# Splitting the weights two row blocks at a time in a two-layer RWKV-7 / forgetting-attention kernel on one core

## The chip, the core and the metric

The kernel runs on one core of one Trainium2 chip. The metric is device time in microseconds (us). Where several executions are told of, their median counts. TensorE is written PE (its weight load PEld), VectorE DVE, ScalarE ACT, GpSimd POOL, and SyncE, which issues most of the transfers, SP.

## What is computed

Two layers on 256 frames of 2048 channels in float32: layer 0 mixes over time with RWKV-7, layer 1 with forgetting attention. Behind each stands a SwiGLU with 5632 hidden channels, and a norm ends the program. Cut to what carries the time:

```
x = x + rwkv7_time_mix(rmsnorm(x), ...)      # k, v, r: 2048x2048 each; LoRAs; recurrence over frames; w_o
x = x + swiglu(rmsnorm(x), w_gu[0], w_d[0])  # (silu(h @ gate) * (h @ up)) @ down
x = x + fox_attention(rmsnorm(x), ...)       # w_in: 2048 x (4*2048 + 96); 32 heads; w_o
x = x + swiglu(rmsnorm(x), w_gu[1], w_d[1])
return rmsnorm(x)
```

The recurrence is `S_t = S_{t-1} diag(w_t) + (S_{t-1} a_t) b_t^T + v_t k_t^T, y_t = S_t r_t` for each of 32 heads of 64 channels.

## The kernel before, in words

Weights are far larger than activations, so every large product holds 128x128 pieces of the activations as the stationary operand and streams weights of 128 rows by 512 columns past them. Matmuls take their operands in a shorter format than float32; to lose nothing, each operand is split exactly in two: `wh` is the weight rounded to the short format, `wl` is the rest (`w - wh`), and likewise for activations (`xh`, `xl`). A block of 128x512 weights then costs, for each of the two halves of the frames, three matmuls: `xh*wh`, `xh*wl`, `xl*wh` (L174, L175, L176), six in all.

The class `Stream` runs the weights. Its plan lists all products in order, 1648 blocks in 828 pieces. A piece is what one transfer brings: two blocks (128x1024, 512 KB), or a single block of 97 rows for the eight products of the decay and in-context-rate LoRAs (`w2`, `a2`). `_load` puts a transfer on SP's queue into one of three staging buffers `st`. `_ensure(p)` is called ahead of the matmuls of block p. It splits all blocks up to p + 6, each with one ACT instruction (L148, rounds `st` to `wh`) and one DVE instruction (L149, `wl = st - wh`), into buffers of one block taken from a ring of seven, then asks for the loads three pieces further on. In the attention layer `deepen` adds two more buffers from a pool `wx`, so that the reach there is p + 8. A staging buffer comes free when the DVE has split its second block; a `wh`/`wl` buffer when the last matmul of its block is done.

All other work is written as generators that advance by one step behind every third matmul (`tick`): norms, transposes, the RWKV-7 recurrence in eight units of 128 frames by 8 heads (`prepare`, `solve`, `merge`, `chain`, `post`), and attention head by head. A scheduler then sets the order on each engine, which is kept strictly. In the recurrence `chain` does, twice per unit, a chain of small matmuls with evictions between them: PE L765/L767, ACT L770 (`vu`), PE L773, ACT L775 (`vu`), PE L778/L780, then DVE L785 or L787/L788 (the new state `sv`) and ACT L789 (`Y`).

At the entrance of the attention layer five tiny transfers (L990 `bf`, L993 and L994 `gains`, 0.1 to 0.2 KB each) go on POOL's queue. L995 on the DVE scales `gains`. Two larger ones (L1003, 384 KB each) go on ACT's queue.

Of the kernel before, what the change touches and what calls it, by code (L numbers as in the profile page):

```python
# [8 lines left out]
F32 = mybir.dt.float32  # L9
F32R = mybir.dt.float32r  # L10
BF16 = mybir.dt.bfloat16
AF = mybir.ActivationFunctionType
ALU = mybir.AluOpType
# [4 lines left out]
P = 128  # L18
# [4 lines left out]
N = 64  # L23
# [41 lines left out]
class Stream:  # L65
# [1 line left out]


    NS = 3
    NW = 7  # L70

    def __init__(self, tc, ctx, plan, limit):
        self.nc = tc.nc
# [2 lines left out]
        self.stage = ctx.enter_context(tc.tile_pool(name="stage", bufs=self.NS))  # L76
        self.wp = ctx.enter_context(tc.tile_pool(name="wp", bufs=self.NW))
        self.psm = ctx.enter_context(tc.tile_pool(name="psm", bufs=4, space=PSUM))
# [52 lines left out]
            self.raw[self.loaded] = st  # L131
            self.loaded += 1

    def _ensure(self, p):

        nc = self.nc
        last = min(p + self.NW - 1 + 2 * (self.extra is not None), len(self.blocks) - 1)
        while self.halved <= last:
            i, j, n, rows, end = self.blocks[self.halved]
            self._load(i)  # L140
            st = self.raw[i][:rows, j * n : (j + 1) * n]
            pool = self.wp
            if self.extra is not None:
                self.turn = (self.turn + 1) % (self.NW + 2)
                pool = self.extra if self.turn < 2 else self.wp
            hi = pool.tile([P, 512], F32R, name="wh")
            lo = pool.tile([P, 512], F32R, name="wl")
            nc.scalar.copy(hi[:rows, :n], st)  # L148
            nc.vector.tensor_tensor(lo[:rows, :n], st, hi[:rows, :n].bitcast(F32), op=ALU.subtract)  # L149
            if end:  # L150
                del self.raw[i]
            self.split[self.halved] = (hi, lo)
            self.halved += 1
        i, _, _, _, end = self.blocks[last]
        self._load(i + self.NS - (not end))

    def gemm(self, name, lhs, ready=None):
        nc = self.nc
        got, _, k, n = self.plan.popleft()
        assert got == name, (got, name)  # L160
        kts = -(-k // P)
        ps = [self.psm.tile([P, 512], F32, name="mm") for _ in range(2)]
        for kt in range(kts):
            self._ensure(self.cur)
            hi, lo = self.split.pop(self.cur)
            self.cur += 1
            if ready is not None:
                self.until(lambda: ready(kt))
            rows = min(P, k - kt * P)
            wh, wl = hi[:rows, :n], lo[:rows, :n]  # L170
            xh, xl = lhs(kt)
            for t in range(2):
                c = slice(t * P, (t + 1) * P)
                nc.tensor.matmul(ps[t][:, :n], xh[:rows, c], wh, start=kt == 0, stop=False)  # L174
                nc.tensor.matmul(ps[t][:, :n], xh[:rows, c], wl, start=False, stop=False)  # L175
                nc.tensor.matmul(ps[t][:, :n], xl[:rows, c], wh, start=False, stop=kt == kts - 1)  # L176
                self.tick()
        return ps
# [20 lines left out]
def hybrid_kernel(ctx, tc, const, x, a_norm_g, a_mix, a_w_rkv, a_w0, a_w1, a_w2, a_a0, a_a1, a_a2,  # L199
                  a_g1, a_g2, a_k_k, a_k_a, a_r_k, a_lnx_g, a_lnx_b, a_w_o, b_norm_g, b_w_in, b_b_f,  # L200
                  b_qn_g, b_kn_g, b_on_g, b_w_o, f_norm_g, f_w_gu, f_w_d, final_g, out):
    nc = tc.nc
# [33 lines left out]
    S = Stream(tc, ctx, plan, 4)  # L236
# [89 lines left out]
    with ExitStack() as actx:  # L326
# [5 lines left out]
        with ExitStack() as bctx:  # L332
            st = bctx.enter_context(tc.tile_pool(name="st1", bufs=1))
# [647 lines left out]
    with ExitStack() as bctx:  # L981
        b1 = bctx.enter_context(tc.tile_pool(name="b1", bufs=1))
        b2 = bctx.enter_context(tc.tile_pool(name="b2", bufs=2))
        S.deepen(bctx.enter_context(tc.tile_pool(name="wx", bufs=2)))
        cdram = dram.tile([H, T], F32, name="cdram")
        oT = pair("xa")
        alpha = b1.tile([P, 2, 2 * H], F32, name="alpha")
        cq = b1.tile([P, 2, H], F32, name="cq")
        bf = b1.tile([H, 1], F32, name="bf")
        nc.gpsimd.dma_start(bf[:, :], b_b_f[0][:, None])  # L990
        gains = b1.tile([P, 2], F32, name="gains")
        for j in range(2):
            nc.gpsimd.dma_start(gains[j * N : j * N + N, 0:1], b_qn_g[0][:, None])  # L993
            nc.gpsimd.dma_start(gains[j * N : j * N + N, 1:2], b_kn_g[0][:, None])  # L994
        nc.vector.tensor_scalar(gains[:, 0:1], gains[:, 0:1], N ** -0.5, None, op0=ALU.mult)  # L995
        nc.vector.tensor_scalar(rsh[:, :], rst[:, :], 0.5, None, op0=ALU.mult)

# [324 lines left out]
```

## Time and profile before

| What | Value |
|---|---|
| three timed runs | 2664.91, 2687.72, 2695.59 us; median 2687.72 |
| the profiled execution | 2667.2 us, its span 2665.4 us |
| mean granted TensorE clock in it | 0.989 |
| PE busy | 2624.3 us, 98% of the span, 15256 matmuls |
| DVE, ACT busy | 1677.5 us (63%), 1478.7 us (55%) |
| POOL busy | 87.9 us (3%) |
| transfers | 468.48 MB, 176 GB/s on the mean |

The span is the time from the first to the last instruction of the profiled execution; the 1.8 us that its own time is longer lie around it. A row of instructions names the line, engine and operation, then out<-in, the shape, the count, the busy time, the mean of one in ns, and the idle time of the engine just before with what ended most of it. A row of a table by stretches gives the stretch, its length, the busy time of each engine with the number of instructions started, the granted clock of TensorE (1.00 is full), the share of the 16 DMA engines and the GB/s. Matmuls are pipelined: a busy time counts each from its start to its modelled end, and starts follow each other faster than that.

### The profile page before, as it was taken

The numbers are of one execution on the slowest core, as the hardware profiler recorded it, in microseconds if no ns is written. First come the engines' busy times: TensorE is split into PE (matmuls) and PEld (weight loads), VectorE is DVE, ScalarE is ACT, GpSimd is POOL, SyncE is SP. The second block draws the span as 40 slices with busy tenths as digits, with TensorE's granted clock in tenths as the row PEclk, the third lists the DMA queues.
The fourth block names the chain that finished last, engine by engine and source line by source line (L and its number), as shares of the span: only waits on it lengthen the run. The fifth ranks groups of instructions, "written<-read, shape, count | busy, mean of one in ns | idle before, by whom it ended". The sixth has DMA issues, their size and how long they took to land.

```text
span 2665.4 us, 41151 instructions
## 1 busy us (share of the span) xinstructions
PE 2624.3 (98%) x15256; PEld 2142.5 (80%) x15256; DVE 1677.5 (63%) x2977; ACT 1478.7 (55%) x2849; POOL 87.9 (3%) x68
## 2 busy tenths in 40 slices
PE   7999999999999999999999999999999999999998
PEld 6788777777888888888888888888888888888886
DVE  7885876766655555555556677776755555555554
ACT  6665676756655545444445565665655555454443
POOL 0000010000000000000000110110000000000000
PEclk9999998889999999999999999999999999999999
DMA  5676332323666666665557666665566666665554
GB/s 187 193 215 206 99 100 79 92 91 111 178 194 185 193 187 191 187 193 191 192 191 205 202 193 184 196 185 170 174 192 186 192 187 191 187 191 193 196 195 157
DMA packets 253946, 468.48 MB, mean 176 GB/s; under 512 B 22248, under 2 KB 32696, under 8 KB 253744
## 3 DMA queue, kind: packets, MB, share of 16 engines
q1 hardware_dynamic: 251056, 464.58, 57.5%
q8 instruction: 120, 1.97, 0.3%
q10 hardware_dynamic: 2528, 1.26, 0.2%
q14 instruction: 82, 0.67, 0.1%
q0 software_dynamic: 160, 0.00, 0.0%
HBM read 457.37 MB, written 4.23 MB: 173 GB/s over the span
## 4 chain that ended last, share of the span: by engine, by line
PE 95%; ACT 2%; DVE 1%; DMA 1%; issue 1%; SPq 0%; ACTq 0%; POOLq 0%; DVEq 0%
PE mm L174 28%; PE mm L176 28%; PE mm L175 28%; PE bg L611 1%; PE bg L765 1%; PE bg L767 1%; DMA st<-in_a_w_rkv_dram 1%; PE bg L941 1%; ACT xb L592 1%; PE bg L773 1%; PE bg L302 1%; PE bg L778 1%; PE bg L780 0%; ACT Bs L811 0%; PE bg L1174 0%
## 5 line engine op out<-in xcount | busy, mean ns | idle before, releaser
L149 DVE TENSOR_TENSOR wl<-st,wh 128x512 fp32r<-128x512 f32 (+1 forms) x1648 | 1130.2, 691 | 823.1 <-ACT wh L148 817.8
L148 ACT CAST wh<-st 128x512 fp32r<-128x512 f32 (+1 forms) x1648 | 1018.8, 623 | 944.9 <-DVE wl L149 695.7
L174 PE MATMUL mm<-wh,xb 128*128 128x512 f32 x2048 | 803.6, 392 | 0.0
L176 PE MATMUL mm<-wh,xb 128*128 128x512 f32 x2048 | 799.8, 391 | 0.0
L175 PE MATMUL mm<-wl,xb 128*128 128x512 f32 x2048 | 799.4, 390 | 0.0
L174 PEld LDWEIGHTS mm<-wh,xb 128*128 128x128 f32 x2048 | 384.6, 188 | 79.9 <-issue 3.3
L176 PEld LDWEIGHTS mm<-wh,xb 128*128 128x128 f32 x2048 | 384.4, 188 | 79.5
L175 PEld LDWEIGHTS mm<-wl,xb 128*128 128x128 f32 x2048 | 384.7, 188 | 76.0
L174 PE MATMUL mm<-wh,xa 128*128 128x512 f32 x768 | 311.2, 406 | 0.0
L175 PE MATMUL mm<-wl,xa 128*128 128x512 f32 x768 | 307.4, 400 | 0.7 <-DVE wl L149 0.7
L176 PE MATMUL mm<-wh,xa 128*128 128x512 f32 x768 | 306.0, 399 | 0.0
L174 PE MATMUL mm<-wh,hb 128*128 128x512 f32 x448 | 174.3, 389 | 0.0
L175 PE MATMUL mm<-wl,hb 128*128 128x512 f32 x448 | 174.3, 389 | 0.0
L176 PE MATMUL mm<-wh,hb 128*128 128x512 f32 x448 | 174.3, 389 | 0.0
L174 PEld LDWEIGHTS mm<-wh,xa 128*128 128x128 f32 x768 | 146.4, 191 | 30.4 <-issue 1.0
L176 PEld LDWEIGHTS mm<-wh,xa 128*128 128x128 f32 x768 | 146.2, 191 | 30.4 <-DVE xa L854 0.2
L175 PEld LDWEIGHTS mm<-wl,xa 128*128 128x128 f32 x768 | 146.6, 191 | 29.2 <-DVE wl L149 1.5
L175 PEld LDWEIGHTS mm<-wl,hb 128*128 128x128 f32 x448 | 84.1, 188 | 17.5
L174 PEld LDWEIGHTS mm<-wh,hb 128*128 128x128 f32 x448 | 84.1, 188 | 17.4
L176 PEld LDWEIGHTS mm<-wh,hb 128*128 128x128 f32 x448 | 84.1, 188 | 17.4
L1122 POOL TENSOR_TENSOR n<-n,pw 128x8 f32<-128x8 f32 x24 | 45.1, 1882 | 411.4 <-DVE n L1121 411.4
L315 DVE TENSOR_TENSOR x<-mm,x 128x512 f32<-128x512 f32 x58 | 38.0, 685 | 11.6 <-PE mm L176 11.5
(277 smaller groups left out, 2007.7 us busy)
## 6 DMA issues: line engine op xcount, KB each, us to landing
st<-in_f_w_gu_dram SPq DMA_DIRECT2D x352, 512.0 KB
st<-in_f_w_d_dram SPq DMA_DIRECT2D x176, 512.0 KB
st<-in_b_w_in_dram SPq DMA_DIRECT2D x128, 512.0 KB
st<-in_a_w_rkv_dram SPq DMA_DIRECT2D x96, 512.0 KB
st<-in_a_w_o_dram SPq DMA_DIRECT2D x32, 512.0 KB
st<-in_b_w_o_dram SPq DMA_DIRECT2D x32, 512.0 KB
x<-in_x_dram SPq DMA_DIRECT2D x16, 256.0 KB
cb<-cdram SPq DMA_DIRECT2D x4, 1024.0 KB
```

The lines of the kernel that those rows point to most:

```text
L148: nc.scalar.copy(hi[:rows, :n], st)
L149: nc.vector.tensor_tensor(lo[:rows, :n], st, hi[:rows, :n].bitcast(F32), op=ALU.subtract)
L174: nc.tensor.matmul(ps[t][:, :n], xh[:rows, c], wh, start=kt == 0, stop=False)
L175: nc.tensor.matmul(ps[t][:, :n], xh[:rows, c], wl, start=False, stop=False)
L176: nc.tensor.matmul(ps[t][:, :n], xl[:rows, c], wh, start=False, stop=kt == kts - 1)
L302: nc.tensor.transpose(tp[:, i * T + t * P : i * T + (t + 1) * P], src[:, t, c : c + P], ident)
L315: nc.vector.tensor_tensor(X[g][:, t, :], ps[t][:, :], X[g][:, t, :], op=ALU.add)
L592: nc.scalar.copy(dst, tpv[half[q], :, c, :])
L611: mm(pm[:, h * P : (h + 1) * P], fkb[us, b * 4 + h, :], far[us, b * 4 + h, :], start=True, stop=True)
L765: mm(pb[us, hs], M[:, c * 8 + h, C : 2 * C], sv[:, hs], start=True, stop=True)
L767: mm(pb[vs, hs], far[us, h, 0:C], sv[us, hs], start=h == 0, stop=False)
L1122: nc.gpsimd.tensor_tensor(n8[:, :], n8[:, :], pw[:, :], op=ALU.pow)
```

## The change

1. A split instruction takes a whole piece: 128x1024 in one ACT and one DVE instruction. `_ensure(i)` now goes by pieces; it is called ahead of each block of piece i and splits up to piece i + 3, then asks for the load of piece i + 6.
2. The ring holds four buffers of 128x1024 (`NW = 4`) where it held seven of 128x512. In the attention layer one more of that size is added where there were two small ones.
3. The five tiny transfers at the attention layer's entrance go on ACT's queue.
4. The program is built with `dynamic_dma_scratch_size=1024`, a smaller ring for POOL's transfers.

```diff
-    NW = 7
+    NW = 4
...
-    def _ensure(self, p):
+    def _ensure(self, i):
...
-        last = min(p + self.NW - 1 + 2 * (self.extra is not None), len(self.blocks) - 1)
+        last = min(i + self.NW - 1 + (self.extra is not None), len(self.pieces) - 1)
         while self.halved <= last:
-            i, j, n, rows, end = self.blocks[self.halved]
-            self._load(i)
-            st = self.raw[i][:rows, j * n : (j + 1) * n]
+            self._load(self.halved)
+            _, _, cnt, n, rows = self.pieces[self.halved]
+            st = self.raw.pop(self.halved)[:rows, : cnt * n]
...
-            hi = pool.tile([P, 512], F32R, name="wh")
-            lo = pool.tile([P, 512], F32R, name="wl")
-            nc.scalar.copy(hi[:rows, :n], st)
-            nc.vector.tensor_tensor(lo[:rows, :n], st, hi[:rows, :n].bitcast(F32), op=ALU.subtract)
+            hi = pool.tile([P, 1024], F32R, name="wh")
+            lo = pool.tile([P, 1024], F32R, name="wl")
+            nc.scalar.copy(hi[:rows, : cnt * n], st)
+            nc.vector.tensor_tensor(lo[:rows, : cnt * n], st, hi[:rows, : cnt * n].bitcast(F32), op=ALU.subtract)
...
-        i, _, _, _, end = self.blocks[last]
-        self._load(i + self.NS - (not end))
+        self._load(last + self.NS)
...
-            self._ensure(self.cur)
-            hi, lo = self.split.pop(self.cur)
+            i, j, _, _, end = self.blocks[self.cur]
+            self._ensure(i)
+            hi, lo = self.split[i]
+            if end:
+                del self.split[i]
...
-            wh, wl = hi[:rows, :n], lo[:rows, :n]
+            wh, wl = hi[:rows, j * n : (j + 1) * n], lo[:rows, j * n : (j + 1) * n]
...
-        S.deepen(bctx.enter_context(tc.tile_pool(name="wx", bufs=2)))
+        S.deepen(bctx.enter_context(tc.tile_pool(name="wx", bufs=1)))
...
-        nc.gpsimd.dma_start(bf[:, :], b_b_f[0][:, None])
+        nc.scalar.dma_start(bf[:, :], b_b_f[0][:, None])
...
-            nc.gpsimd.dma_start(gains[j * N : j * N + N, 0:1], b_qn_g[0][:, None])
-            nc.gpsimd.dma_start(gains[j * N : j * N + N, 1:2], b_kn_g[0][:, None])
+            nc.scalar.dma_start(gains[j * N : j * N + N, 0:1], b_qn_g[0][:, None])
+            nc.scalar.dma_start(gains[j * N : j * N + N, 1:2], b_kn_g[0][:, None])
...
-    nc = _bacc.Bacc("TRN2", target_bir_lowering=False, num_devices=1)
+    nc = _bacc.Bacc("TRN2", target_bir_lowering=False, num_devices=1, dynamic_dma_scratch_size=1024)
```

Because the scheduler sets the order anew, instructions move on every engine. Three places matter below.

The first is ACT at the start of the program, from the last statistics of the input (L281) to the first rounded activations `xa` (L363), on which the first matmuls of the weights wait. L380 evicts the transposed input. Before:

```order
L281 ACTIVATE jk_138,ss<-x_81 128x512
L148 CAST wh<-st 128x512 x4
L380 ACTIVATE hT<-bg,gcol 128x256 x2
L148 CAST wh<-st 128x512 x2
L380 ACTIVATE hT<-bg,gcol 128x256 x4
L363 CAST xa_148<-xmf 128x256
L148 CAST wh<-st 128x512
```

and with the change:

```order
L281 ACTIVATE jk_138,ss<-x_81 128x512
L148 CAST wh<-st 128x1024 x2
L380 ACTIVATE hT<-bg,gcol 128x256 x2
L148 CAST wh<-st 128x1024
L380 ACTIVATE hT<-bg,gcol 128x256 x5
L148 CAST wh<-st 128x1024
L363 CAST xa_148<-xmf 128x256 x3
```

Six blocks stood ahead of the first `xa`, and now eight (four pairs), with one more L380.

The second is ACT in one step of the recurrence, from the eviction of the row weights `wc` (L539) through the chain's evictions L770, L775 and L789. Before:

```order
L539 ACTIVATE wc<-bg 64x8 x2
L844 COPY x_4127<-bg 128x4x128
L871 COPY gt_4667<-mm 128x512
L770 COPY vu<-bg 64x512
L548 ACTIVATE WW<-WW 128x512
L775 COPY vu<-bg 64x512
L148 CAST wh<-st 128x512 x5
L789 COPY Y<-bg 64x512
```

and with the change:

```order
L539 ACTIVATE wc<-bg 64x8 x2
L844 COPY x_3767<-bg 128x4x128
L871 COPY gt_4295<-mm 128x512
L770 COPY vu<-bg 64x512
L548 ACTIVATE WW<-WW 128x512
L148 CAST wh<-st 128x1024
L775 COPY vu<-bg 64x512
L148 CAST wh<-st 128x1024
L789 COPY Y<-bg 64x512
```

Here a pair has moved in front of L775. Over the whole recurrence, of the 48 evictions L770, L775 and L789, 29 stood directly behind a split before, and 19 do now.

The third is ACT at the entrance of the attention layer. With the change:

```order
L148 CAST wh<-st 128x1024 x19
L990 DMA bf<-in_b_b_f_dram 32x1
L281 ACTIVATE jk_12650,ss<-x_6992 128x512
L281 ACTIVATE jk_12652,ss<-x_6992 128x512
L993 DMA gains<-in_b_qn_g_dram 64x1
L994 DMA gains<-in_b_kn_g_dram 64x1
L993 DMA gains<-in_b_qn_g_dram 64x1
L994 DMA gains<-in_b_kn_g_dram 64x1
L148 CAST wh<-st 128x1024 x2
L1003 DMA cb<-in_b_w_in_dram 128x8x96 x2
```

The five tiny transfers stood on POOL between two norms; now they stand on ACT, ahead of the next two pairs.

More of the change, by code (lines that the diff above doesn't have):

```diff
@@ L132, in _load @@
             self.loaded += 1
-    def _ensure(self, p):
+    def _ensure(self, i):
         nc = self.nc
-        last = min(p + self.NW - 1 + 2 * (self.extra is not None), len(self.blocks) - 1)
+        last = min(i + self.NW - 1 + (self.extra is not None), len(self.pieces) - 1)
         while self.halved <= last:
-            i, j, n, rows, end = self.blocks[self.halved]
-            self._load(i)
-            st = self.raw[i][:rows, j * n : (j + 1) * n]
+            self._load(self.halved)
+            _, _, cnt, n, rows = self.pieces[self.halved]
+            st = self.raw.pop(self.halved)[:rows, : cnt * n]
             pool = self.wp
             if self.extra is not None:
-                self.turn = (self.turn + 1) % (self.NW + 2)
-                pool = self.extra if self.turn < 2 else self.wp
-            hi = pool.tile([P, 512], F32R, name="wh")
-            lo = pool.tile([P, 512], F32R, name="wl")
[L148 to L151, printed above, removed]
+                self.turn = (self.turn + 1) % (self.NW + 1)
+                pool = self.wp if self.turn else self.extra
+            hi = pool.tile([P, 1024], F32R, name="wh")
+            lo = pool.tile([P, 1024], F32R, name="wl")
+            nc.scalar.copy(hi[:rows, : cnt * n], st)
+            nc.vector.tensor_tensor(lo[:rows, : cnt * n], st, hi[:rows, : cnt * n].bitcast(F32), op=ALU.subtract)
             self.split[self.halved] = (hi, lo)
             self.halved += 1
-        i, _, _, _, end = self.blocks[last]
-        self._load(i + self.NS - (not end))
+        self._load(last + self.NS)
     def gemm(self, name, lhs, ready=None):
```

## The prediction

> **What bounds the kernel now.** I read the stages first: the table by stretches, one row each for the products k and v with the start (to 250 us), the recurrence (to 655), the first SwiGLU (to 1415), attention (to 1900), the second SwiGLU (to 2653) and the end.
>
> ```profile
> 0.00:250.00 250.00, 230.02 (x1109) 190.56 (x1110) 189.29 (x399) 151.70 (x313) 4.18 (x10) 0.99 0.66 201
> 250.00:655.00 405.00, 395.93 (x4946) 305.29 (x4946) 291.85 (x621) 275.29 (x679) 32.98 (x25) 0.94 0.31 95
> 655.00:1415.00 760.00, 759.91 (x3422) 626.67 (x3421) 428.28 (x643) 388.43 (x652) 0.70 (x1) 1.00 0.63 190
> 1415.00:1900.00 485.00, 484.99 (x2406) 397.94 (x2405) 346.83 (x690) 283.24 (x575) 48.59 (x30) 1.00 0.63 191
> 1900.00:2653.00 753.00, 753.00 (x3379) 622.03 (x3378) 416.84 (x620) 376.07 (x624) 0.70 (x1) 1.00 0.62 187
> 2653.00:2665.00 12.00, 0.41 (x2) 0.00 (x0) 4.42 (x10) 3.96 (x8) 0.70 (x1) 0.74 0.47 175
> ```
>
> The columns are PE, PEld, DVE, ACT, POOL, then the clock. From 655 to 2653 us PE stands for 0.1 us in 1998. But a busy time counts modelled ends, so "busy" doesn't yet say that PE sets the pace: a PE that is fed too slowly could look the same. The timeline of the first SwiGLU, PE, ACT and DVE, seems to say just that:
>
> ```profile
> 1199.55 0.69 DVE L149 TENSOR_TENSOR wl<-st,wh 128x512 fp32r<-128x512 f32 x1 [0.67 <-ACT wh L148]
> 1199.83 0.39 PE L176 MATMUL mm<-wh,hb 128*128 128x512 f32 x1
> 1200.06 0.39 PE L174 MATMUL mm<-wh,hb 128*128 128x512 f32 x1
> ...
> 1200.26 0.62 ACT L148 CAST wh<-st 128x512 fp32r<-128x512 f32 x1 [0.73 <-DVE wl L149]
> ...
> 1200.91 0.69 DVE L149 TENSOR_TENSOR wl<-st,wh 128x512 fp32r<-128x512 f32 x1 [0.67 <-ACT wh L148]
> ...
> 1201.19 0.39 PE L176 MATMUL mm<-wh,hb 128*128 128x512 f32 x1
> ...
> 1201.62 0.62 ACT L148 CAST wh<-st 128x512 fp32r<-128x512 f32 x1 [0.73 <-DVE wl L149]
> ```
>
> ACT, DVE, ACT alternate without a gap in 1201.62 - 1200.26 = 1.36 us, and the six matmuls of a block, L176 to L176, take 1201.19 - 1199.83 = 1.36 us too. If the split were the limit, wider splits would speed up three quarters of the program. The counts decide between the two. Up to 900 us these starts of L174, then of L148:
>
> ```profile
> 0.00:900.00 900.00, 343.95 (x857) 163.20 (x858) 0.97 0.50 150
> 0.00:900.00 900.00, 267.55 (x435) 0.97 0.50 150
> ```
>
> 857 L174 at two per block mean that block 429 is in work; split 435 is in work. Six ahead is all that seven buffers allow, so the splits wait for PE to free a buffer, and the DVE named there only ended at the same moment. PE's own pace, 1.36/6 = 0.227 us per matmul, sets these stages, and the change leaves every matmul as it is: 1648 blocks x 1.36 = 2241 us of the 2665 can't move. Who waits on PE for a split at all is one row in the whole list of waits:
>
> ```profile
> PE mm L175 <- DVE wl L149: 0.7, 1, 0.7
> ```
>
> What remains open is 0 to 250 us, the recurrence with 405 - 395.9 = 9.1 us of idle PE and a mean clock of 0.94, and the entrances of stages.
>
> **The change part by part.** *The price of a pair.* The trace holds a DVE operation of 128x1024, and for ACT casts of two widths:
>
> ```profile
> L149 DVE TENSOR_TENSOR wl<-st,wh 128x512 fp32r<-128x512 f32 x1640 | 1124.7, 691 | 820.9 <-ACT wh L148 815.6
> L1215 DVE TENSOR_TENSOR cb<-cb,cst 128x1024 f32<-128x1024 f32 x8 | 9.7, 1207 | 4.1 <-DMA cb<-cdram 4.1
> L148 ACT CAST wh<-st 128x512 fp32r<-128x512 f32 x1640 | 1013.9, 623 | 942.5 <-DVE wl L149 694.2 <-PE mm L176 183.6 <-DMA st<-in_b_w_in_dram 33.2
> L1011 ACT CAST qT<-cb 128x768 fp32r<-128x768 f32 x2 | 1.6, 843 | 0.0
> ```
>
> DVE: about 1207 ns for a pair against 2 x 691 = 1382, 175 saved. ACT: 843 - 623 = 220 ns per 256 columns, so 1063 for 1024 against 1246, 183 saved. With 820 pairs the busy time falls by 144 us on the DVE and 150 us on ACT. Back to back less is gained, since durations overlap there:
>
> ```profile
> 1485.37 3.09 DVE L149 TENSOR_TENSOR wl<-st,wh 128x512 fp32r<-128x512 f32 x5
> 1481.31 2.70 ACT L148 CAST wh<-st 128x512 fp32r<-128x512 f32 x5
> ```
>
> (3.09 - 0.69)/4 = 0.60 and (2.70 - 0.62)/4 = 0.52 us from start to start, that is 0.09 and 0.10 hidden per instruction, and about 0.08 us saved per pair on each.
>
> *Steady stages (655 to 2653 us): 0.* PE hides all of it. Does the new ring still feed PE? A split began six blocks = 8.16 us ahead of its use and took 0.62 + 0.69 + 0.03 = 1.34: 6.8 us to spare. A pair begins three pieces of 2.72 us ahead, 8.16 again, and takes 1.063 + 1.207 + 0.03 = 2.30: 5.9 us. A staging buffer, once split, has the rest of its round of three pieces for its next load: 8.16 - 2.30 = 5.9 us, where it was 8.16 - 1.36 - 1.34 = 5.5. Both covers hold; if a load came 1 us late every piece, the ring would be empty after six pieces and each further piece would cost that 1 us.
>
> *The start: +1.2 us.* The first matmuls of k wait for `xa` behind the splits on ACT and DVE:
>
> ```profile
> 15.85 1.14 ACT L148 CAST wh<-st 128x512 fp32r<-128x512 f32 x2 [1.22 <-DMA st<-in_a_w_rkv_dram]
> 19.74 1.14 ACT L148 CAST wh<-st 128x512 fp32r<-128x512 f32 x2
> 20.77 1.58 ACT L380 ACTIVATE hT<-bg,gcol 128x256 f32<-128x256 f32 x4
> 22.21 0.43 ACT L363 CAST xa<-xmf 128x256 fp32r<-128x256 f32 x1
> ...
> 23.18 0.48 PE L174 MATMUL mm<-wh,xa 128*128 128x512 f32 x1
> ```
>
> Six blocks stood ahead of that L363, now four pairs and one L380 more: on ACT 4 x 1.063 - 6 x 0.623 = +0.5, and an L380 of 0.4; on the DVE 4 x 1.207 - 6 x 0.691 = +0.7, and two small operations. That gives 0.9 to 1.5 us. From below, 0 (ACT has idle time there, waiting for the load); from above +3, both engines in a row.
>
> *The recurrence: +2 us.* The rows of L148 and of L149 in 250 to 655 us:
>
> ```profile
> 250.00:655.00 405.00, 68.46 (x114) 0.94 0.31 95
> 250.00:655.00 405.00, 76.31 (x113) 0.94 0.31 95
> ```
>
> 114 splits, 8 of them the single blocks of `w2` and `a2`, become 53 pairs and 8 singles: 53 x 0.183 = 9.7 us less on ACT, 53 x 0.175 = 9.3 less on the DVE, which are busy 275 and 292 us there. That is 3% less queueing, and of PE's 9.1 idle us 3% is 0.3. Against it each pair is a longer obstacle. ACT's evictions of the chain wait for PE, not for ACT:
>
> ```profile
> ACT vu L770 <- PE bg L767: 36.4, 11, 6.0
> ACT vu L775 <- PE bg L773: 26.3, 16, 4.0
> ACT Y L789 <- PE bg L780: 16.9, 10, 4.7
> ```
>
> so splits fill holes. By the order, 29 of the 48 stood directly behind a split, 29 x 0.62 = 18.0 us at most; now 19, 19 x 1.063 = 20.2: +2.2. I take the sum, +2. From below: all idle goes, -9. From above, the second rival, +38.
>
> *The entrance of attention: 0.* On POOL the tiny transfers cost a wait on the DVE:
>
> ```profile
> 1415.63 0.69 POOL L990 DMA_DIRECT2D bf<-in_b_b_f_dram x1 [728.95 <-DVE wl L149]
> 1423.58 0.15 DVE L995 TENSOR_SCALAR gains<-gains 128x1 f32<-128x1 f32 x1 [3.64 <-DMA gains<-in_b_qn_g_dram]
> gains<-in_b_qn_g_dram POOLq DMA_DIRECT2D x2, 0.2 KB, 5.5
> 1416.66 0.39 ACTq L1003 DMA_DIRECT2D cb<-in_b_w_in_dram  x1
> ```
>
> On ACT five issues of 0.39 us, 2.0 us in all, delay the two pairs behind them; `bf` also waits there until its space is free, which came at 1415.6, when the first SwiGLU ended. The stall of 3.6 us on the DVE goes or shrinks. The 5.9 us in front of PE cover the 2.0. Without that cover 2 us would be lost, and if weight loads on SP had to wait for these transfers to land (5.5 us by that row), 5.5. Below, nothing: PE has no gap there to win. POOL's smaller ring has no user left.
>
> The sum: 2665.4 + 1.2 + 2 + 0 = 2668.6 us of span, 2670.4 of time, 3 us over the profiled execution. That one lies 20 us under the median of the timed runs, which spread over 31 us by themselves. The middle of all four executions is (2667.2 + 2687.7) / 2 = 2677.5; with the 3 us, **2681 us**. About 1% is what a measurement of this kernel can tell from no change, and this is 0.3%.
>
> **The rivals.** *Faster: the recurrence tightens (2648 us).* If lighter ACT and DVE queues let the chain run without gaps, PE's 9 idle us go, and the clock could stay full: 0.94 over 405 us is 24 us. Together -33. For it: DVE and ACT are 72% and 68% busy there. Against: 3% less load is little, and the clock falls where PE is over 97% busy:
>
> ```profile
> 350.00:400.00 50.00, 48.96 (x674) 1.00 0.36 111
> 400.00:450.00 50.00, 49.20 (x611) 0.87 0.22 70
> 500.00:550.00 50.00, 49.12 (x560) 0.73 0.24 73
> ```
>
> The Trainium skill (TensorE: Matmul & The Clock Gate, Part 1: The HAM clock gate) has the clock at half after an idle window of about 3.4 us. These rows don't show such idleness: 0.8 us of 50 at a clock of 0.87, 1.0 us at 1.00. By that rule fewer gaps would win the 24 us; by the rows nothing ties the two.
>
> *Slower: pairs in front of the chain (2719 us).* The recurrence is one chain through PE, ACT and DVE in order. If every step of it found a pair ahead, 48 evictions would come 1.063 - 0.623 = 0.44 us later, 21 us, and 16 state updates on the DVE, two instructions each, 0.52 us per instruction, 17 us: +38. It takes a loss of 27 us, seven steps in ten, to be 1% slower. Against: 19 evictions stand behind a pair, not 48. The Trainium skill (Perfetto Trace Analysis, Optimizing Scalar/DVE Operations) says that where ACT and DVE aren't saturated but cause bubbles on others, breaking instructions up may let work end sooner; that speaks against pairs here. The trace agrees on the first half only: they aren't saturated, and PE's bubbles are 9 us in 405.
>
> *The split was the limit after all (2585 us).* Were the alternation of 1.36 us what paces PE, pairs at 2.30 per 2.72 us would free up to 0.21 us per block, over the 1376 blocks of attention and the SwiGLUs 289 us in the extreme; a third of it, 96 us, would give 2585. The counts (six ahead, the full ring) exclude it but for a misreading.
>
> **How the numbers follow.** My forecast, no change that can be measured: 0.74. The faster recurrence 0.13, the split as limit 0.02: faster 0.15. The pairs in the way 0.11: slower. The predicted time is the forecast's, 2681. Its own range: below, -9 of the recurrence; above, 3 + 2 + 5.5 = 11 of the parts; and the four executions lie from 13 us below their middle to 18 above it. If all goes one way that is 2677.5 - 9 - 13 = 2656 to 2677.5 + 11 + 18 = 2706. Below I reach on to the first rival's 2648; the slower rival's 2719 and the split as limit stay outside.
>
> **What would show it.** Right: L148 and L149 at 128x1024 with about 1060 and 1210 ns, 820 of each; the stages from 655 to 2653 us as long as before within 3 us; six L174 to L176 still in 1.36 us; splits counted in blocks still 6 to 8 ahead of L174. The first L174 at about 24.3 us (before 23.2). DVE L995 waiting less. Wrong: a stretch of the SwiGLUs shorter by tens of us (then the split was the limit), waits of PE on `wh` or `wl` in the steady stages (then the ring is too short), or a recurrence off 405 us by more than 10 at the same clock.

## The result: 0.8% slower, with the largest loss in attention, where the forecast had none

| | before | after |
|---|---|---|
| median of 20 runs each | 2674.78 us (2664.91 to 2695.59) | 2695.57 us (2681.19 to 2713.26) |
| ratio after/before, 95% interval | | 1.0077 [1.0056, 1.0099] |
| profiled execution, its span, granted clock | 2667.2, 2665.4 us, 0.989 | 2692.75, 2691.0 us, 0.985 |
| DVE, ACT busy | 1677.5, 1478.7 us | 1570.1, 1331.6 us |

The median rose by 20.8 us; the forecast had 3 on top of its base.

**A measure without the clock.** Runs of one kernel lie 30 us apart, so stages can't be compared by length alone. The product of span and mean granted clock helps; it is called the product below. Two runs of the changed kernel had spans of 2679.4 and 2711.5 us at mean granted clocks of 0.989 and 0.978: span times clock is 2650 and 2652. Over its 20 runs the product has a median of 2650.2 (2646 to 2657); over 96 runs of the kernel before, taken beside the experiments, 2636.9 (2632 to 2640). (One more execution of the kernel before, of 8386.67 us, is left out.) The runs of one kernel thus differ by the clock and by little else, and with it taken out the change costs 13.3 us. The rest of the 20.8 lies in the mean clock (0.9839 against 0.9854, 4 us of span) and in the scatter of medians. Below, "clock-free" is a length less the time that a clock under 1 took from it (at half clock, half the time).

The table by stretches, first two rows of the kernel before (recurrence and attention), cut where the first matmul of the same block starts in both kernels. The columns are PE, PEld, DVE, ACT, POOL, the clock, DMA share and GB/s:

```profile
253.00:657.70 404.70, 395.54 (x4946) 304.67 (x4945) 293.02 (x623) 275.86 (x680) 32.98 (x25) 0.94 0.31 95
...
1415.20:1923.40 508.20, 508.19 (x2519) 416.69 (x2518) 364.37 (x721) 300.03 (x612) 48.59 (x30) 1.00 0.63 190
```

and the stages of the changed kernel behind the start: the products of layer 0, the recurrence, the first SwiGLU, attention, the second SwiGLU:

```profile
24.50:253.70 229.20, 224.56 (x1072) 185.46 (x1071) 171.98 (x299) 128.51 (x218) 3.42 (x5) 0.99 0.65 198
253.70:666.30 412.60, 399.57 (x4945) 308.66 (x4943) 292.84 (x571) 270.36 (x629) 34.85 (x25) 0.93 0.31 95
666.30:1424.60 758.30, 758.27 (x3408) 626.84 (x3409) 382.59 (x365) 332.73 (x375) 0.70 (x1) 1.00 0.62 189
1424.60:1948.20 523.60, 515.52 (x2519) 420.11 (x2518) 349.05 (x561) 274.94 (x452) 45.55 (x25) 0.99 0.61 185
1948.20:2677.20 729.00, 729.00 (x3260) 603.24 (x3260) 357.88 (x326) 308.83 (x326) 0.70 (x1) 1.00 0.62 187
```

| stage | before, clock-free | after, clock-free | difference | lost to the clock, before and after |
|---|---|---|---|---|
| first matmul of the weights to the recurrence | 228.1 | 227.4 | -0.7 | 1.7, 1.7 |
| recurrence | 380.8 | 383.7 | +2.9 | 23.9, 29.0 |
| first SwiGLU | 757.5 | 758.3 | +0.8 | 0, 0 |
| attention | 508.3 | 518.5 | +10.2 | 0, 5.1 |
| second SwiGLU | 728.5 | 728.9 | +0.4 | 0, 0 |

With the first matmul, 1.3 us later (23.2 to 24.5 us), the stages of these two executions differ by 14.9; the product gave 13.3 over all runs. Attention holds two thirds of it: DVE and ACT are less busy there than before, by 15 and 25 us, and PE, which stood for 0.01 us in 508, now stands for 523.60 - 515.52 = 8.1.

**Where PE stands.** The list of waits in attention of the changed kernel (engine, line, releaser: total, times, longest), rows left out:

```profile
ACT wh L148 <- DMA st<-in_b_w_in_dram: 57.9, 40, 4.8
...
ACT sc L1165 <- DVE nm L1164: 48.1, 16, 7.3
...
DVE k L1127 <- POOL n L1122: 13.6, 8, 1.8
ACT wh L148 <- DMA st<-in_b_w_o_dram: 11.3, 8, 3.0
DVE x L1127 <- POOL n L1122: 11.3, 8, 1.8
...
DVE o L1127 <- POOL n L1122: 7.9, 5, 1.8
...
PE bg L1174 <- ACT sc L1165: 6.3, 10, 2.4
```

and the same rows of the kernel before:

```profile
ACT wh L148 <- DMA st<-in_b_w_in_dram: 33.2, 24, 3.0
ACT sc L1165 <- DVE nm L1164: 26.6, 15, 2.0
...
DVE x L1127 <- POOL n L1122: 6.1, 8, 1.8
...
DVE k L1127 <- POOL n L1122: 4.1, 5, 1.1
...
ACT wh L148 <- DMA st<-in_b_w_o_dram: 3.6, 3, 1.9
...
DVE o L1127 <- POOL n L1122: 2.3, 5, 0.9
```

Splits now wait 69.2 us for their loads, where it was 36.8. PE isn't stopped by a missing split, though, but by attention's own work: L1174 transposes the scores that L1161, L1164 (DVE) and L1165 (ACT) make. How a late load gets there is read from the timeline of the changed kernel, ACT, DVE and PE ahead of the longest stop:

```profile
1741.89 1.05 ACT L148 CAST wh<-st 128x1024 fp32r<-128x1024 f32 x1 [1.64 <-DMA st<-in_b_w_in_dram]
```
```profile
1742.97 1.23 DVE L149 TENSOR_TENSOR wl<-st,wh 128x1024 fp32r<-128x1024 f32 x1 [1.46 <-ACT wh L148]
1744.12 0.74 DVE L1161 SCALAR_TENSOR_TENSOR sc<-bg,cq,cb 128x128 f32<-128x128 f32 x2
1744.97 1.23 DVE L149 TENSOR_TENSOR wl<-st,wh 128x1024 fp32r<-128x1024 f32 x1
1746.11 0.60 DVE L1164 TENSOR_REDUCE nm<-sc 128x1 f32<-128x128 f32 x2
```
```profile
1746.43 0.40 ACT L1165 ACTIVATE sc<-sc,nm 128x128 f32<-128x128 f32 x1 [1.49 <-DVE nm L1164]
```
```profile
1746.97 0.33 PE L1174 MATMUL bg<-cst,sc 128*128 128x128 f32 x1 [2.40 <-ACT sc L1165]
```

The load is late by 1.64 us, the ACT split with it, the DVE's split behind that by 1.46, and L1161 stands behind it in the DVE's order; L1164 then stands behind one more pair, and PE stops for 2.40 us. Why was the load late? Some 40 us earlier the DVE stood three times for POOL, with splits queued behind (DVE's timeline, then ACT's):

```profile
1697.35 0.69 DVE L1127 TENSOR_TENSOR x<-x,n 128x512 f32<-128x512 f32 x1 [1.53 <-POOL n L1122]
...
1698.67 0.17 DVE L1121 TENSOR_SCALAR n<-n 128x8 f32<-128x8 f32 x1
1700.66 0.69 DVE L1127 TENSOR_TENSOR k<-k,n 128x512 f32<-128x512 f32 x1 [1.81 <-POOL n L1122]
1701.27 1.22 DVE L149 TENSOR_TENSOR wl<-st,wh 128x1024 fp32r<-128x1024 f32 x1
...
1705.49 0.69 DVE L1127 TENSOR_TENSOR k<-k,n 128x512 f32<-128x512 f32 x1 [1.82 <-POOL n L1122]
```
```profile
1694.73 1.05 ACT L148 CAST wh<-st 128x1024 fp32r<-128x1024 f32 x1 [1.31 <-DMA st<-in_b_w_in_dram]
```

The pair that ACT rounded from 1694.73 on was finished by the DVE at 1701.27 + 1.22 = 1702.49: 7.8 us in which its staging buffer couldn't be filled again, against 2.30 without anything between. So the transfers fell to half their rate, two loads of 512 KB short in 12 us, and when they ran again splits stood waiting for them (the table by stretches, its last columns DMA share and GB/s; then ACT's timeline, and SP's):

```profile
1697.00:1703.00 6.00, 6.00 (x30) 4.97 (x29) 3.80 (x7) 1.66 (x3) 1.95 (x2) 1.00 0.27 84
1703.00:1709.00 6.00, 5.73 (x27) 4.45 (x26) 4.15 (x7) 2.55 (x5) 1.64 (x1) 1.00 0.34 93
1709.00:1715.00 6.00, 6.00 (x28) 4.95 (x27) 3.04 (x4) 4.98 (x7) 0.00 (x0) 1.00 0.81 261
```
```profile
1719.91 1.05 ACT L148 CAST wh<-st 128x1024 fp32r<-128x1024 f32 x1 [3.41 <-DMA st<-in_b_w_in_dram]
1724.52 1.05 ACT L148 CAST wh<-st 128x1024 fp32r<-128x1024 f32 x1 [3.56 <-DMA st<-in_b_w_in_dram]
```
```profile
1714.27 0.53 SPq L1096 DMA_DIRECT2D prev<-v  x1
...
1718.20 0.54 SPq L1098 DMA_DIRECT2D prev<-v  x1
```

These two waits have a second part: between the loads SP also issues attention's own transfers `prev<-v`, about as many bytes as one load. The loads that it issued at 1713.85 and 1716.26 us came only at 1719.9 and 1724.5, after 6 and 8 us. The kernel before has the same transfers, and beside them waits of 1.48 and 1.94 us.

ACT waits of 1.5 us for loads go on from there to the late one at 1741.89. The starts, counted as in the prediction, show one lasting shortage: the splits were 8 blocks ahead of the matmuls at 1694.8 us, 5 at 1708.6, 4 at 1724.6, and no more than 6 until PE stopped. In the same part of the kernel before (1680 to 1726 us) they stayed 7 to 9 ahead.

Why does the DVE stand longer for POOL, 32.8 us in its three rows against 12.5? Each of 24 steps is L1121 on the DVE, L1122 on POOL, then L1127 on the DVE. If they are matched in order, a split stands between L1121 and its L1127 in 22 of the 24 before, and in 8 now. A split in that place costs the DVE little, since it would stand for POOL anyway. The step at 1698.67 above has nothing between; one from the kernel before:

```profile
1481.25 0.16 DVE L1121 TENSOR_SCALAR n<-n 128x8 f32<-128x8 f32 x1
...
1482.04 0.68 DVE L149 TENSOR_TENSOR wl<-st,wh 128x512 fp32r<-128x512 f32 x1
...
1483.16 0.69 DVE L1127 TENSOR_TENSOR k<-k,n 128x512 f32<-128x512 f32 x1 [0.36 <-POOL n L1122]
```

That POOL's waits began this shortage is read from the trace; no run takes them away alone. Behind the stop the clock is at half for 10.2 us, the 5.1 us of the table:

```profile
1748.00:1751.40 3.40, 2.70 (x8) 2.00 (x8) 1.30 (x2) 2.14 (x8) 0.00 (x0) 0.50 0.65 183
1751.40:1758.20 6.80, 6.80 (x27) 5.48 (x27) 1.62 (x3) 0.98 (x1) 0.00 (x0) 0.53 0.44 138
```

The theory for the experiments: with three staging buffers and pairs, loads come late in attention, and the late splits hold up attention's own work in the strict order. Its rivals: the moved transfers or POOL's ring (run 1 against 2), the longer reach in attention (run 8), and a cause in the clock, by way of the shorter reach of the ring (runs 9 and 10).

### The profile page after: what moved, and what is told of

It is laid out like the page before. It is cut to its first block, busy times and chain, and to the rows that moved or that the text cites. A ratio compares the mean times of both kernels' runs of the same rounds, so it can differ in the third digit from the quotient of the medians.

```text
span 2691.0 us, 38804 instructions
## 1 busy us (share of the span) xinstructions
PE 2636.5 (98%) x15256; PEld 2152.9 (80%) x15256; DVE 1570.1 (58%) x2157; ACT 1331.6 (49%) x2029; POOL 86.8 (3%) x63
## 4 chain that ended last, share of the span: by engine, by line
PE 84%; DVE 5%; DMA 5%; ACT 3%; issue 2%; POOL 1%; SPq 0%; ACTq 0%; POOLq 0%; DVEq 0%
PE mm L174 25%; PE mm L176 24%; PE mm L175 24%; DVE wl L149 2%; DMA st<-in_b_w_in_dram 2%; PE bg L611 1%; PE bg L765 1%; POOL n L1122 1%; ACT wh L148 1%; PE bg L767 1%; DMA cb<-cdram 1%; PE bg L941 1%; DMA st<-in_a_w_rkv_dram 1%; PE bg L773 1%; ACT xb L592 1%
## 5 line engine op out<-in xcount | busy, mean ns | idle before, releaser
L149 DVE TENSOR_TENSOR wl<-st,wh 128x1024 fp32r<-128x1024 f32 (+1 forms) x828 | 1008.0, 1218 | 887.2 <-ACT wh L148 885.4
L148 ACT CAST wh<-st 128x1024 fp32r<-128x1024 f32 (+1 forms) x828 | 866.8, 1048 | 1024.7 <-PE mm L176 908.1
L174 PE MATMUL mm<-wh,xb 128*128 128x512 f32 x2048 | 806.7, 394 | 0.0
L175 PE MATMUL mm<-wl,xb 128*128 128x512 f32 x2048 | 798.7, 390 | 1.3 <-DVE wl L149 1.3
L174 PEld LDWEIGHTS mm<-wh,xb 128*128 128x128 f32 x2048 | 385.2, 188 | 80.2 <-issue 4.0
L175 PEld LDWEIGHTS mm<-wl,xb 128*128 128x128 f32 x2048 | 385.4, 188 | 78.9 <-DVE wl L149 2.7
L174 PE MATMUL mm<-wh,xa 128*128 128x512 f32 x768 | 312.4, 407 | 1.5 <-ACT xa L853 1.5
L175 PE MATMUL mm<-wl,xa 128*128 128x512 f32 x768 | 306.8, 399 | 2.6 <-DVE wl L149 2.5
L174 PE MATMUL mm<-wh,hb 128*128 128x512 f32 x448 | 174.3, 389 | 0.0
L175 PE MATMUL mm<-wl,hb 128*128 128x512 f32 x448 | 174.3, 389 | 0.0
L174 PEld LDWEIGHTS mm<-wh,xa 128*128 128x128 f32 x768 | 147.0, 191 | 32.7 <-ACT xa L853 1.9
L175 PEld LDWEIGHTS mm<-wl,xa 128*128 128x128 f32 x768 | 147.3, 192 | 31.4 <-DVE wl L149 3.3
L175 PEld LDWEIGHTS mm<-wl,hb 128*128 128x128 f32 x448 | 84.1, 188 | 17.5
L174 PEld LDWEIGHTS mm<-wh,hb 128*128 128x128 f32 x448 | 84.1, 188 | 17.3
L1122 POOL TENSOR_TENSOR n<-n,pw 128x8 f32<-128x8 f32 x24 | 44.9, 1869 | 430.9 <-DVE n L1121 430.9
```

What stands on the lines that cost most here:

```text
L148: nc.scalar.copy(hi[:rows, : cnt * n], st)
L149: nc.vector.tensor_tensor(lo[:rows, : cnt * n], st, hi[:rows, : cnt * n].bitcast(F32), op=ALU.subtract)
L1122: nc.gpsimd.tensor_tensor(n8[:, :], n8[:, :], pw[:, :], op=ALU.pow)
```

## The experiments

Medians are of 8 to 12 runs. The ratios against the kernel before, with their 95% interval, are not the quotients of the medians (its own lie there from 2674.9 to 2676.5 us; in run 4 the medians give 1.0058 and the ratio is 1.0038). The product of span and clock stands beside each median, since it separates 3 us where the median can't.

**1. The transfers alone.** The kernel before, with parts 3 and 4 of the change.

```diff
-        nc.gpsimd.dma_start(bf[:, :], b_b_f[0][:, None])
+        nc.scalar.dma_start(bf[:, :], b_b_f[0][:, None])
...
-    nc = _bacc.Bacc("TRN2", target_bir_lowering=False, num_devices=1)
+    nc = _bacc.Bacc("TRN2", target_bir_lowering=False, num_devices=1, dynamic_dma_scratch_size=1024)
```

> The kernel before with only the five tiny transfers moved to ACT's queue and POOL's ring smaller; splits stay 128x512 in seven buffers. The change measured 1.0077 of before. If wide splits are the cause (width), 0.998 to 1.002 of before and attention (first to last block of its products, 800 to 1120 in the count of blocks, 508 us before, 523.6 in the change) within 2 us of before. If the transfers or their order on ACT are the cause, 1.004 or more.

Measured: 2677.35 us, 1.0003 [0.9971, 1.0035]; product 2635.0; attention 507.6 clock-free. The transfers and the ring cost nothing.

**2. The pairs with the transfers on POOL.** The changed kernel with the five transfers back on POOL's queue.

```diff
-        nc.scalar.dma_start(bf[:, :], b_b_f[0][:, None])
+        nc.gpsimd.dma_start(bf[:, :], b_b_f[0][:, None])
...
```

> The change with the five tiny transfers back on POOL's queue (the smaller ring stays, for space). Width, late loads or buffers by pairs as the cause: 1.005 to 1.010 of before, attention over 516 us. The transfers as the cause: 0.998 to 1.002.

Measured: 2696.47 us, 1.0082 [1.0053, 1.0111]; product 2650.3; attention 517.8. The whole loss is there without the moved transfers: it comes from the pairs.

**3. Half-width splits in buffers of a pair.** The changed kernel; each piece is split in two instructions of 512 on ACT and two on the DVE, and all else stays by pairs.

```diff
-            nc.scalar.copy(hi[:rows, : cnt * n], st)
-            nc.vector.tensor_tensor(lo[:rows, : cnt * n], st, hi[:rows, : cnt * n].bitcast(F32), op=ALU.subtract)
+            for c in [slice(j * n, (j + 1) * n) for j in range(cnt)]:
+                nc.scalar.copy(hi[:rows, c], st[:, c])
+                nc.vector.tensor_tensor(lo[:rows, c], st[:, c], hi[:rows, c].bitcast(F32), op=ALU.subtract)
```

> The change, but each piece is split by two ACT and two DVE instructions of 128x512 into its buffer of 128x1024; reach and release by pieces stay. If the width of an instruction that others stand behind is the cause: 0.998 to 1.003 of before. If buffers that come free by pairs, or the reach counted in pieces, are the cause: 1.005 to 1.010, as the change.

Measured: 2693.16 us, 1.0053 [1.0027, 1.0078]; product 2644.9; attention by stretches, and its waits for loads (lines from there on are one number higher):

```profile
1448.70:1958.10 509.40, 508.23 (x2519) 417.33 (x2518) 360.62 (x721) 290.62 (x612) 41.89 (x25) 1.00 0.62 190
```
```profile
ACT wh L149 <- DMA st<-in_b_w_in_dram: 40.4, 27, 3.8
```

PE's idle time in attention falls from 8.1 to 1.2 us and the stage to 509.4, although DVE and ACT are 12 and 16 us busier in it: there the width of the instruction, with the order that goes with it, makes the difference. Over the whole kernel only 5 of the 13 us of the product come back, and by the ratio the second theory's forecast came true, so the width isn't all (the profiled execution has a product of 2640, at the low end of its runs). The mean clock of 0.983 keeps the median high.

**4. Four staging buffers.** The changed kernel with one more.

```diff
-    NS = 3
+    NS = 4
```

> The change with four staging buffers in place of three, so that each load is asked for one piece earlier. If loads that come late, since a staging buffer is held until a whole pair is split, are the cause: 0.998 to 1.002 of before, and ACT's waits for loads of in_b_w_in in attention well under the change's. If the width alone is the cause: 1.005 to 1.010, attention over 516 us.

Measured: 2692.08 us, 1.0038 [1.0014, 1.0062]; product 2639.8. Attention, and its waits for loads of `in_b_w_in`:

```profile
1447.80:1957.00 509.20, 508.44 (x2520) 417.20 (x2519) 348.67 (x561) 274.74 (x452) 45.50 (x25) 1.00 0.62 190
```
```profile
ACT wh L148 <- DMA st<-in_b_w_in_dram: 11.1, 10, 2.9
```

Pairs as wide as in the changed kernel, the same three rows of the DVE standing for POOL (13.6, 11.3 and 7.9 us), but loads that are there: attention takes 509.2, and 10.4 of the 13.3 us of the product are back. In attention late loads are the link that decides; wide splits and POOL's waits do little harm without it. The ratio lies between the two forecasts, though, and the median falls by 3.5 us only: these runs had a mean clock of 0.9825 where the change had 0.9839, about 4 us, and the rest is scatter.

**5 and 6. One engine wide.** The changed kernel with ACT wide and the DVE in halves (5), and the other way (6).

```diff
-            nc.vector.tensor_tensor(lo[:rows, : cnt * n], st, hi[:rows, : cnt * n].bitcast(F32), op=ALU.subtract)
+            for c in [slice(j * n, (j + 1) * n) for j in range(cnt)]:
+                nc.vector.tensor_tensor(lo[:rows, c], st[:, c], hi[:rows, c].bitcast(F32), op=ALU.subtract)
```
```diff
-            nc.scalar.copy(hi[:rows, : cnt * n], st)
+            for c in [slice(j * n, (j + 1) * n) for j in range(cnt)]:
+                nc.scalar.copy(hi[:rows, c], st[:, c])
```

> The change with ACT's rounding in one instruction of 128x1024 per piece and the DVE's subtraction in two of 128x512. Attention took 508.3 us before, 518.5 in the change without the clock's share, 509.4 with both engines at half width. If what counts is that the strict order on the DVE holds wide splits among attention's own operations, attention is 508 to 511 us and span times clock 2640 to 2646. If it is how long a staging buffer is held (1.05 + 0.6 + 0.69 = 2.3 us, as in the change), 516 to 520 and 2648 to 2652.

> The change with two ACT instructions of 128x512 per piece and one DVE instruction of 128x1024. Both theories of the last run expect attention at 515 to 520 us here (wide on the DVE; a buffer held 0.62 + 0.52 + 1.22 = 2.4 us); if ACT's width alone mattered, 508 to 511.

Measured: with ACT wide 2686.35 us, 1.0042 [1.0019, 1.0065], product 2640.7, attention 513.2; with the DVE wide 2691.84 us, 1.0069 [1.0042, 1.0097], product 2647.4, attention 514.5. Neither engine's width alone carries the loss. In attention the first lies between the figures of the two theories (its product is in the first theory's range), the second just under the expected one; both fit in with the waits for loads (the table below), so I take no more from them. PE stands at another place in these two, at the transposes of attention's gated output (L303 for DVE L1238, 4.3 and 5.4 us).

**7. Single blocks with four staging buffers.** Run 1's kernel with `NS = 4`: if late loads cost time, the kernel before may lose some too.

```diff
-    NS = 3
+    NS = 4
```

> Splits of one block in seven buffers as before, transfers on ACT and the smaller ring as in the change, and four staging buffers. If a fourth staging buffer only makes good what the pairs spoilt: 0.997 to 1.003 of before, span times clock 2633 to 2638. If late loads cost the kernel before something as well: 2625 to 2632.

Measured: 2667.16 us, 0.9971 [0.9944, 0.9998]; product 2633.5. In attention the waits for loads are nearly gone, 4.6 us in all, and PE is busy for all of its 507.6 us. By the product the first theory was right. It is faster than the kernels before and after the change, than the one before by little: 3.4 us of the product, at a mean clock of 0.988.

**8. No longer reach in attention.** The changed kernel without the fifth buffer.

```diff
-        S.deepen(bctx.enter_context(tc.tile_pool(name="wx", bufs=1)))
```

> The change without the fifth pair buffer in attention: a reach of eight blocks there, where before had nine and the change has ten. If loads that come late are the cause, less reach does not mend it: attention 516 us or more (without the clock's share). If the longer reach, which puts more splits ahead of attention's own operations, is the cause: 508 to 512.

Measured: 2693.96 us, 1.0071 [1.0039, 1.0103]; product 2649.8; attention 516.9. A shorter reach doesn't mend it, so the loss doesn't need the longer one. PE stops elsewhere here, though, for the splits themselves (L175 for `wl`, 6.4 us), so this run doesn't tell what the longer reach does by itself.

**9. Five pairs.** A ring of five pairs all through, without the extra one.

```diff
-    NW = 4
+    NW = 5
...
-        S.deepen(bctx.enter_context(tc.tile_pool(name="wx", bufs=1)))
```

> The change with five pair buffers throughout in place of four and a fifth in attention alone. Attention keeps its reach: 516 to 520 us without the clock's share. The kernels with pair buffers granted TensorE a mean clock of 0.982 to 0.984 over their runs, those with single buffers 0.985 to 0.988. If the shorter reach in the recurrence, where pieces of one block fill a whole pair buffer, is what lowers the clock: 0.985 or more here and the recurrence (blocks 144 to 256) at 381 us or less. If not: 0.982 to 0.984 as in the change.

Measured: 2695.56 us, 1.0069 [1.0041, 1.0097]; product 2652.1; attention 518.1; mean clock 0.9846, between the two forecasts; the recurrence 383.0 clock-free in its one profile, as in the change (383.7). A longer ring of pairs wins nothing.

**10. Five single blocks.** Run 1's kernel with a ring of five.

```diff
-    NW = 7
+    NW = 5
```

> Splits of one block in five buffers in place of seven (seven in attention), three staging buffers, transfers on ACT and the smaller ring as in the change. If a reach of four blocks in the recurrence lowers the clock, 0.983 or less on the mean, and 1.003 to 1.007 of before; if not, 0.985 to 0.986 and 0.998 to 1.003. In attention reach alone should cost little: 507 to 511 us.

Measured: 2677.31 us, 1.0004 [0.9978, 1.0029]; product 2638.5; attention 508.4; mean clock 0.9857. With single blocks a much shorter reach costs neither waits nor clock, so the rival of the reach falls for them; for pairs, run 9's clock between the two forecasts leaves a part of it open.

**11 and 12. Around the best.** Run 7's kernel with a ring of eight, and run 1's with five staging buffers (both edits against run 1's kernel).

```diff
-    NS = 3
-    NW = 7
+    NS = 4
+    NW = 8
```
```diff
-    NS = 3
+    NS = 5
```

> Eight buffers of one block, four staging buffers, transfers on ACT, the smaller ring: the best run so far (seven and four: 0.9971) with one block more of reach. If reach matters for the clock: 0.988 or more of clock, 0.993 to 0.997 of before; if not, within 0.002 of 0.997.

> Seven buffers of one block and five staging buffers. With four, ACT's waits for loads in attention are 4.6 us and PE loses nothing to them there; a fifth should win nothing more: 0.995 to 0.999 of before, span times clock 2632 to 2636, attention 507 to 508 us. Under 2630 would say that loads were still late elsewhere.

Measured: 2668.77 us, 0.9966 [0.9935, 0.9997], product 2633.7; and 2668.93 us, 0.9960 [0.9933, 0.9987], product 2630.5. The eighth buffer adds nothing; the fifth staging buffer wins 3 us of the product, a little more than forecast; in the median the three can't be told apart.

**All together**, sorted by the time that splits in attention wait for loads (the rows of `in_b_w_in` and `in_b_w_o` of one profile each), beside the DVE's waits for POOL there (its three rows) and the clock-free length of attention:

| kernel | waits for loads, us | DVE for POOL, us | attention, us |
|---|---|---|---|
| single blocks, five staging buffers (12) | 0 | 14.5 | 507.7 |
| single blocks, four staging buffers (7) | 4.6 | 15.1 | 507.6 |
| the same, a ring of eight (11) | 7.9 | 18.3 | 507.7 |
| pairs, four staging buffers (4) | 16.2 | 32.8 | 509.2 |
| before | 36.8 | 12.5 | 508.3 |
| five single blocks (10) | 37.0 | 12.7 | 508.4 |
| transfers alone (1) | 40.1 | 12.6 | 507.6 |
| pairs in halves (3) | 43.6 | 19.5 | 509.4 |
| ACT wide (5) | 49.3 | 21.9 | 513.2 |
| DVE wide (6) | 53.0 | 27.6 | 514.5 |
| pairs, no longer reach (8) | 63.3 | 32.8 | 516.9 |
| after | 69.2 | 32.8 | 518.5 |
| pairs, transfers on POOL (2) | 74.0 | 32.7 | 517.8 |
| five pairs (9) | 75.9 | 32.8 | 518.1 |

In these profiles up to some 44 us of waits are covered; beyond, the stage grows by about 0.4 us per us. With three staging buffers, more waits for POOL go with more waits for loads; with four, the 32.8 us cost almost nothing. That fits the reading above, but no run changes POOL's waits alone.

**What stays open** is the clock's share. Over 96 runs the eight kernels with buffers of a pair have a mean clock of 0.9834, over 120 runs the three with single blocks and three staging buffers 0.9853: 0.0019 with a standard error of 0.0005, some 5 us. In the one profile of each kernel the loss lies mostly in the recurrence. With single blocks the reach isn't it (run 10), and with pairs it isn't the width (run 3: 0.9831), nor late loads (run 4: 0.9825). No run tells what in the order of a pair kernel lowers it, and the 0.9874 of runs 7, 11 and 12 isn't explained either. It weighs: with four staging buffers in both, pairs (run 4) still have a median 25 us above single blocks (run 7), and 6.3 us of product are the smaller part of it. So the late loads are the cause in attention, and not of the whole 20.8 us.

## Why the prediction was wrong

- **The price of a pair** was right: 1063 and 1207 ns forecast, medians of 1055 and 1225 measured; the groups by line of the changed kernel, whose means hold the eight single blocks too:

```profile
L149 DVE TENSOR_TENSOR wl<-st,wh 128x1024 fp32r<-128x1024 f32 (+1 forms) x828 | 1008.0, 1218 | 887.2 <-ACT wh L148 885.4
L148 ACT CAST wh<-st 128x1024 fp32r<-128x1024 f32 (+1 forms) x828 | 866.8, 1048 | 1024.7 <-PE mm L176 908.1
```

  ACT's splits cost 1013.9 - 866.8 = 147 us less (150 forecast), the DVE's 1124.7 - 1008.0 = 117 (144 forecast).
- **That this busy time is worth nothing, and the split isn't the limit,** was right: the SwiGLUs take 758.3 and 728.9 us against 757.5 and 728.5. The count that decided it holds. The starts of L174, then of L148, up to 900 us in the changed kernel:

```profile
0.00:900.00 900.00, 341.39 (x844) 161.89 (x844) 0.97 0.49 148
0.00:900.00 900.00, 225.51 (x218) 0.97 0.49 148
```

  Block 422 is in work; 218 pieces, eight of them single blocks, are 428 blocks: six ahead, the full ring.
- **The start, +1.2,** was right: the first L174 came at 24.54 us (24.3 forecast, 23.2 before), and 0.7 of it was left at the recurrence.

```profile
24.54 0.47 PE L174 MATMUL mm<-wh,xa 128*128 128x512 f32 x1
```

- **The recurrence, +2,** was right in size: +2.9 clock-free. Its reason, pairs as longer obstacles in front of the chain, isn't shown: ACT waits for PE before the chain's evictions about as long as before, 77.3 us in the three rows against 79.6:

```profile
ACT vu L775 <- PE bg L773: 27.7, 13, 5.3
ACT vu L770 <- PE bg L767: 27.4, 10, 4.9
ACT Y L789 <- PE bg L780: 22.2, 13, 4.2
```

  In one profile of each kernel the recurrence takes from 377.4 to 381.7 us clock-free with single blocks and from 379.6 (run 4) to 386.8 (run 6) with pairs, so a difference of 2.9 is little more than their scatter, and the size may be luck. By the wall it took 8 us more; 5 of these are the clock, for which the sum had no term, and whose cause is open.
- **The entrance of attention, 0,** was right: from block 800 to block 816 it took 29.1 us before and 28.5 after, the DVE's wait at L995 is gone, and run 1 has no loss.
- **The step that failed is "Steady stages (655 to 2653 us): 0"**, and in it "Both covers hold". It measured +10.2 us in attention, and 5.1 more by the clock behind the stop. The covers of 5.9 us were computed with DVE and ACT free for the next split at once. That is true of the SwiGLUs. In attention the strict order puts norms, scores and waits for POOL between the splits. A load takes 4.1 us from issue to landing, the median in the changed kernel:

```profile
st<-in_b_w_in_dram SPq DMA_DIRECT2D x128, 512.0 KB, 4.1
```

  so 5.9 - 4.1 = 1.8 us was the room left for all of these, and a single wait of the DVE for POOL is 1.8. The cover alone doesn't tell the kernels apart, though: by the same sum the kernel before had less, 5.5 - 4.1 = 1.4 (with the same 4.1, since its page gives none), and the forecast was that the change has more room. What the sum left out is what stands between two splits, and that changed: with pairs the order leaves POOL's pauses empty, 32.8 us of the DVE against 12.5, and the splits' waits for loads went from 36.8 to 69.2. The same paragraph named the danger ("if a load came 1 us late every piece") and didn't look at whether loads came late already: the rows of before with 33.2 and 3.6 us of waits in attention were the sign that this one of the steady stages had the least room. The second part of the error is what to watch: "waits of PE on `wh` or `wl`" hardly exist (1.3 us in attention). PE waits on L1165, behind a late split in another engine's order.
- **The slower rival** had the right mechanism, pairs standing in front of other work in the order, and the wrong place: it was priced for the chain of the recurrence, where the rows above show none of it. The rule of the Trainium skill (Perfetto Trace Analysis, Optimizing Scalar/DVE Operations), that breaking instructions up may let work end sooner where DVE and ACT aren't saturated but cause bubbles on others, holds in attention: run 3 has 27 us more of busy time on the two and a stage 9.1 us shorter.
- **The base.** The middle of four executions, 2677.5, lay 2.7 us over the median of 20. The other 20.8 - 3.2 = 17.6 us are missing terms: attention's 10.2, some 4 for the clock, and scatter. The median of 2695.57 lies inside the stated 2648 to 2706, but by luck: the range was that wide for the scatter of four executions and for waits at attention's entrance that didn't come. "No change that can be measured" was wrong, since the interval of the ratio, 1.0056 to 1.0099, excludes 1.

## What to carry to other kernels

Fewer, wider instructions on an engine that isn't the bound save busy time that nobody waits for; what they can cost is how long they hold a buffer and what stands behind them in a strict order. Compute a ring's cover stage by stage, with every instruction and every wait that the order puts between two refills, and look for the stage where loads already come late: in this kernel an extra staging buffer was worth more there than a cheaper split. When runs of one kernel spread with the clock, compare span times clock before comparing medians.

## What was not expected of the hardware

- Runs of one kernel differ by up to 40 us (2656.7 to 2696.7 over the 96 runs of the kernel before), and span times clock by 8: with the one execution of 8386.67 us left out, the granted clock is nearly the whole of the scatter.
- In the profiles, stretches at half clock have lengths of 3.4 us and its multiples (10.2 us from 1748 us on, behind the stop; 3.4, 6.8, 10.2 and 20.5 us in the recurrence before). In attention, where the clock is full otherwise, PE's stop of 2.40 us with shorter ones behind it was followed by 10.2 us at half clock, 5.1 us of loss beyond the stop itself.
